# Summing four partial modulation rows with two-column selection matmuls, in place of transposes and a VectorE reduction

## The chip, the cores and the metric

One core of one Trainium2 chip runs the whole program. The time is device microseconds (us) of one execution; beside it stands the profile of one execution, whose span runs from its first to its last instruction. Everything is float32. The weight matrices are split into a high and a low part of a reduced float32 type, so that three fast matmuls stand in for one exact one; the modulation alone uses plain float32 matmuls.

## The reference, cut to what matters

Two layers of a diffusion backbone, 512 latent and 128 context tokens of width 1024. Each layer is modulated by a condition vector: `c` for latent tokens, `c_ctx` for context tokens.

```python
def modulation(cond, w_ada_l, b_ada_l):
    m = jnp.einsum('bd,de->be', jax.nn.silu(cond), w_ada_l) + b_ada_l
    shift, scale, gate = jnp.split(m, 3, axis=-1)
...
    h = x * (1.0 + scale) + shift
    y = mixer(h, ...)               # projections, two attentions, a gated scan, one output projection
    x = layer_norm(DEEPNORM_ALPHA * x + gate * y, ...)
```

`w_ada_l` is 1024 x 3072. What the change touches is how the 3072 values of `m`, for both conditions, come to stand down the 128 partitions, where shift and scale are used.

## The kernel before, in words

The 3072 columns are cut into 12 chunks of 256 for each layer, `j` = 0 to 11 (0 to 3 are shift, 4 to 7 scale, 8 to 11 gate). Chunks 0 to 7 of layer 0 are worked off in pairs at the start (`mod_start`, L1314); the other 16 chunks (4 of layer 0, 12 of layer 1) run later, one at a time, between the projection chunks of the two layers.

For one of these 16, `mod_next` (L297) multiplies the condition (two columns, padded to 32) with the 256 weight columns. The 1024 rows are eight blocks of 128; block `k` goes to the partition group `k % 4` of 32 partitions, and only two blocks are summed in each group. So PSUM holds four partial sums, in the partitions 32q and 32q+1, of two rows of 256 each. ScalarE copies them to `ms` (L305). A later step, `mod_end` (L325), calls `mod_out` (L309): it has to add the four partial sums and turn the row of 256 into two columns of 128 partitions. `mod_out` is called with one chunk at a time, so `n` is 2 in each call.

`mod_start` does the same for its chunks with `sel_c`, a constant of 128 x 2 that is 1 in column c for each partition p with p % 32 == c:

```python
        for i in range(4):
            mm(out=pm[:, 256 + 2 * i:258 + 2 * i], lhsT=ms[:, i // 2, 128 * (i % 2):128 * (i % 2) + 128], rhs=sel_c,
               start=True, stop=True)
```

What it writes is read from PSUM by the `stt` (scalar_tensor_tensor on VectorE, L1323) that adds the bias and stores shift or scale.

The order of the work: generators yield at steps that are priced by hand (`COST`), `drive` picks the next one, and the weight chunks with the modulation chunks between them are the background stream (`bg_stream`, L725, with `MODS` and `ORDER`). `mod_end` of a chunk is called from `flush`, at the end of the next projection chunk or ahead of the next modulation chunk. The framework then writes out a queue for each engine, in which instructions of neighbouring steps may change places; each engine works off its queue in that order. PSUM tiles named `pB` share three banks.

Of the kernel before, what the change touches and what calls it, by code (L numbers as in the profile page):

```python
# [8 lines left out]
F32 = mybir.dt.float32  # L9
# [3 lines left out]
ALU = mybir.AluOpType  # L13
AX = mybir.AxisListType
# [59 lines left out]
def hybrid_kernel(ctx: ExitStack, tc: tile.TileContext, A, cst, outs):  # L74
    nc = tc.nc
# [3 lines left out]
    small = ctx.enter_context(tc.tile_pool(name="small", bufs=2))  # L79
# [5 lines left out]
    def gran(shape=(128, T), dt=F32, name="g"):  # L85
        t = gp.tile(list(shape), dt, tag="g", name=name)
        return t
# [23 lines left out]
    def bankB():  # L111
        return bank("B")
# [10 lines left out]
    mm = nc.tensor.matmul  # L123
    act = nc.scalar.activation
    dve = nc.vector
    tt = nc.vector.tensor_tensor
    stt = nc.vector.scalar_tensor_tensor
# [28 lines left out]
    ident = cs[:, C_ID:C_ID + 128]  # L156
# [3 lines left out]
    sel_c = cs[:, C_SC:C_SC + 2]  # L160
# [126 lines left out]
    modt = [[const.tile([128, KB, 2], F32, name=f"mod{l}{i}") for i in range(3)] for l in range(L)]  # L287
# [21 lines left out]
    def mod_out(l, parts):  # L309
        pm = bankB()  # L310
        n = 2 * len(parts)
        for i in range(n):
            ms = parts[i // 2][1][:, 128 * (i % 2):128 * (i % 2) + 128]
            nc.tensor.transpose(pm[:, 128 * i:128 * i + 128], ms, ident)
        sm = small.tile([128, 4, 2], F32, tag="sm", name="sm")
        v = pm.rearrange("p (i q c) -> p i c q", i=4, q=4)[:, 0:n, 0:2, :]
        dve.tensor_reduce(out=sm[:, 0:n], in_=v, axis=AX.X, op=ALU.add)
        for i, (j, _) in enumerate(parts):
            k0 = 2 * (j % 4)
            b0 = V_BA + 24 * l + 2 * j  # L320
            stt(out=modt[l][j // 4][:, k0:k0 + 2, :], in0=sm[:, 2 * i:2 * i + 2],
                scalar=1.0 if j // 4 == 1 else 0.0, in1=vv[:, b0:b0 + 2].unsqueeze(2).to_broadcast([128, 2, 2]),
                op0=ALU.add, op1=ALU.add)

    def mod_end(l, j, ms):  # L325
        mod_out(l, [(j, ms)])
        if j == 7 and l > 0:
            lg, lb = (vv[:, V_LN + 8 * i:V_LN + 8 * i + 8].unsqueeze(2).to_broadcast([128, KB, 2]) for i in range(2))
            tmp = small.tile([128, KB, 2], F32, tag="lnf", name="lnf", bufs=1)
            tt(out=tmp, in0=scale[l], in1=lb, op=ALU.mult)  # L330
            tt(out=shift[l], in0=shift[l], in1=tmp, op=ALU.add)
            tt(out=scale[l], in0=scale[l], in1=lg, op=ALU.mult)
        if j == 11:
            gt = small.tile([128, 2, KB], F32, tag="gt", name="gt", bufs=1)
            dve.tensor_copy(gt, modt[l][2].rearrange("p k c -> p c k"))
            ps = bankC()
            nc.tensor.transpose(ps[0:16, 0:128], gt.rearrange("p c k -> p (c k)"), ident)
            gr = small.tile([16, 128], F32, tag="gr", name="gr", bufs=1)
            dve.tensor_copy(gr, ps[0:16, 0:128])
            nc.sync.dma_start(out=g_scr[l].rearrange("c (k p) -> (c k) p", p=128), in_=gr)  # L340
# [987 lines left out]
    with in_order(nc.scalar.engine, nc.vector.engine, nc.tensor.engine):  # L1328
        for j in range(4):
# [8 lines left out]
            for k in range(KB):  # L1338
                q = k % 4
                mm(out=ps[32 * q:32 * q + 32], lhsT=sc[:, k, :], rhs=rw[k].rearrange("p s c -> p (s c)"),  # L1340
                   start=(k < 4), stop=(k >= 4))
            ms = gran((128, 2, 256), name="ms0")
# [15 lines left out]
            for i in range(2):  # L1358
                k = 2 * j + i
# [95 lines left out]
```

## Time and profile before

| what | us |
|---|---|
| median of three runs (lowest, highest) | 952.72 (952.40, 954.18) |
| the profiled execution, its own time | 954.79 |
| its span, first to last instruction | 953.0 |
| TensorE busy (PE), and weight loads (PEld) | 901.2, 749.7 |
| VectorE (DVE), ScalarE (ACT), GpSimd (POOL) busy | 596.5, 582.1, 79.3 |

A busy PE is one with a matmul in flight; matmuls overlap, so what a matmul costs is the distance from its start to the start of the next one, not its duration. A plain weight load (LDWEIGHTS) and a matmul (MATMUL) make a pair. The chain that ended last is followed back from the last instruction: its pieces add up to the span, and work outside of it had slack.

### The profile page before, as it was taken

The numbers are of one execution on the slowest core, as the hardware profiler recorded it, in microseconds if no ns is written. First come the engines' busy times: TensorE is split into PE (matmuls) and PEld (weight loads), VectorE is DVE, ScalarE is ACT, GpSimd is POOL, SyncE is SP. The second block draws the span as 40 slices with busy tenths as digits, with TensorE's granted clock in tenths as the row PEclk, the third lists the DMA queues.
The fourth block names the chain that finished last, engine by engine and source line by source line (L and its number), as shares of the span: only waits on it lengthen the run. The fifth ranks groups of instructions, "written<-read, shape, count | busy, mean of one in ns | idle before, by whom it ended". The sixth has DMA issues, their size and how long they took to land.

```text
span 953.0 us, 20559 instructions
## 1 busy us (share of the span) xinstructions
PE 901.2 (95%) x8213; PEld 749.7 (79%) x8213; DVE 596.5 (63%) x1340; ACT 582.1 (61%) x1309; POOL 79.3 (8%) x113
## 2 busy tenths in 40 slices
PE   6999999999999999999999999999989989999995
PEld 3798877887777758678989997878768867777895
DVE  2355557756777865343697466785587795544467
ACT  2335677567776867773265368656877676877311
POOL 0000002000001010200023000020000100210012
PEclk8899999999999999999999999999999999999998
DMA  9946521344431212215614452114124122114222
GB/s 291 315 139 177 150 88 37 104 138 112 128 92 53 91 32 69 70 51 186 208 67 151 114 153 86 29 45 120 51 78 122 47 69 54 51 45 133 77 91 99
DMA packets 103617, 100.37 MB, mean 105 GB/s; under 512 B 9449, under 2 KB 91873, under 8 KB 103521
## 3 DMA queue, kind: packets, MB, share of 16 engines
q1 hardware_dynamic: 103520, 99.05, 35.0%
q8 instruction: 65, 1.06, 0.5%
q14 instruction: 32, 0.25, 0.1%
HBM read 77.25 MB, written 6.31 MB: 88 GB/s over the span
## 4 chain that ended last, share of the span: by engine, by line
PE 70%; DVE 12%; ACT 7%; DMA 7%; issue 2%; SPq 1%; POOL 0%; DVEq 0%; ACTq 0%; POOLq 0%
PE pA L373 8%; PE pA L375 8%; PE pA L374 8%; PE pO L1146 7%; PE pA L394 5%; PE pS L1023 5%; PE pA L395 5%; PE pA L396 5%; DMA wraw<-in_w_in_dram 4%; DMA Q<-Q 2%; PE pS L1027 2%; PE pB L1082 2%; PE pB L1080 2%; PE pB L1079 2%; ACT pS L1031 1%
## 5 line engine op out<-in xcount | busy, mean ns | idle before, releaser
L1030 DVE TENSOR_REDUCE nmx<-pS 128x1 f32<-128x640 f32 x128 | 105.4, 823 | 119.9 <-PE pS L1023 65.3
L373 PE MATMUL pA<-wh,mh 128*128 128x256 f32 x600 | 171.0, 285 | 1.3 <-DVE gate_t L409 1.3
L375 PE MATMUL pA<-wh,ml 128*128 128x256 f32 x600 | 170.3, 284 | 0.0
L374 PE MATMUL pA<-wl,mh 128*128 128x256 f32 x600 | 170.0, 284 | 0.0
L1031 ACT ACTIVATE pS<-pS,nmx 128x640 f32<-128x640 f32 x128 | 98.2, 767 | 50.4 <-DVE nmx L1030 47.5
L260 ACT CAST wh<-wraw 128x512 fp32r<-128x512 f32 x140 | 83.7, 619 | 73.4 <-PE pA L375 31.9
L261 DVE TENSOR_TENSOR wl<-wraw,wh 128x512 fp32r<-128x512 f32 x140 | 92.8, 689 | 39.8 <-ACT wh L260 39.0
L373 PEld LDWEIGHTS pA<-wh,mh 128*128 128x128 f32 x600 | 114.7, 191 | 3.6 <-DVE gate_t L409 2.0
L375 PEld LDWEIGHTS pA<-wh,ml 128*128 128x128 f32 x600 | 114.6, 191 | 1.7 <-issue 1.2
L374 PEld LDWEIGHTS pA<-wl,mh 128*128 128x128 f32 x600 | 114.7, 191 | 1.1 <-issue 0.8
L1088 ACT ACTIVATE PT<-pB 128x512 f32<-128x512 f32 x160 | 89.1, 599 | 27.0 <-PE pB L1080 14.7
L394 PE MATMUL pA<-mh,wh 128*128 128x320 f32 x224 | 71.6, 320 | 0.0
L394 PE MATMUL pA<-hh,wh 128*128 128x320 f32 x224 | 70.6, 315 | 0.7 <-DVE gate_t L409 0.7
L395 PE MATMUL pA<-ml,wh 128*128 128x320 f32 x224 | 70.8, 316 | 0.0
L396 PE MATMUL pA<-mh,wl 128*128 128x320 f32 x224 | 70.6, 315 | 0.0
L396 PE MATMUL pA<-hh,wl 128*128 128x320 f32 x224 | 69.7, 311 | 0.0
L395 PE MATMUL pA<-hl,wh 128*128 128x320 f32 x224 | 69.5, 310 | 0.0
L1146 PE MATMUL pO<-PT,tk 128*64 128x512 f32 x256 | 64.9, 613 | 0.4 <-ACT PT L1088 0.3
L373 PE MATMUL pA<-wh,hh 128*128 128x256 f32 x200 | 57.6, 288 | 0.0
L375 PE MATMUL pA<-wh,hl 128*128 128x256 f32 x200 | 57.0, 285 | 0.0
L374 PE MATMUL pA<-wl,hh 128*128 128x256 f32 x200 | 56.8, 284 | 0.0
L394 PEld LDWEIGHTS pA<-mh,wh 128*128 128x128 f32 x224 | 43.2, 193 | 2.5 <-issue 1.8
(297 smaller groups left out, 1966.3 us busy)
## 6 DMA issues: line engine op xcount, KB each, us to landing
wraw<-in_w_ada_dram SPq DMA_DIRECT2D x32, 512.0 KB, 4.5
wraw<-in_w_in_dram SPq DMA_DIRECT2D x30, 512.0 KB, 4.6
wraw<-in_w_in_dram SPq DMA_DIRECT2D x48, 256.0 KB, 3.4
wa<-in_w_ada_dram SPq DMA_DIRECT2D x32, 256.0 KB, 5.4
wraw<-in_w_out_dram SPq DMA_DIRECT2D x16, 512.0 KB, 3.5
Q<-Q SPq DMA_DIRECT2D x32, 160.0 KB, 2.6
KD<-dkh SPq DMA_DIRECT2D x32, 96.0 KB, 3.2
QD<-dqh SPq DMA_DIRECT2D x32, 80.0 KB, 3.2
```

The source lines that it names most:

```text
L260: nc.scalar.copy(hi[n], src)
L261: tt(out=lo[n], in0=src, in1=hi[n].bitcast(F32), op=ALU.subtract)
L373: mm(out=ps[:, o:o + 256], lhsT=hi[k][:, sl], rhs=a, start=(n == 0), stop=False)
L374: mm(out=ps[:, o:o + 256], lhsT=hi[k][:, sl], rhs=b, start=False, stop=False)
L375: mm(out=ps[:, o:o + 256], lhsT=lo[k][:, sl], rhs=a, start=False, stop=(n == last))
L394: mm(out=ps, lhsT=wa, rhs=hi[k][:, sl], start=(k == 0), stop=False)
L395: mm(out=ps, lhsT=wa, rhs=lo[k][:, sl], start=False, stop=False)
L396: mm(out=ps, lhsT=wb, rhs=hi[k][:, sl], start=False, stop=(k == KB - 1))
L1030: dve.tensor_reduce(out=nmx[:, t, i:i + 1], in_=sv, axis=AX.XY, op=ALU.max, negate=True)
L1031: act(sv, sv, AF.Exp, bias=nmx[:, t, i:i + 1], accum_out=den[:, t, i:i + 1])
L1088: return pt, act(pt, ps, AF.Exp).ins
L1146: x = mm(out=o[64 * (i % 2):64 * (i % 2) + 64], lhsT=value(k, i % 2), rhs=pt, start=k == 0, stop=k == 4)
```

## The change

`mod_out` no longer transposes the two blocks of 128 columns of `ms` into 128 columns of PSUM each and sums four of them on VectorE. It multiplies each block with `sel_c`, so that TensorE makes the sum of the four groups, two columns for each block, and the `stt` reads these columns from PSUM. `sm` and the reduction are gone.

```diff
         pm = bankB()
         n = 2 * len(parts)
         for i in range(n):
-            ms = parts[i // 2][1][:, 128 * (i % 2):128 * (i % 2) + 128]
-            nc.tensor.transpose(pm[:, 128 * i:128 * i + 128], ms, ident)
-        sm = small.tile([128, 4, 2], F32, tag="sm", name="sm")
-        v = pm.rearrange("p (i q c) -> p i c q", i=4, q=4)[:, 0:n, 0:2, :]
-        dve.tensor_reduce(out=sm[:, 0:n], in_=v, axis=AX.X, op=ALU.add)
+            mm(out=pm[:, 2 * i:2 * i + 2], lhsT=parts[i // 2][1][:, 128 * (i % 2):128 * (i % 2) + 128], rhs=sel_c,
+               start=True, stop=True)
         for i, (j, _) in enumerate(parts):
             k0 = 2 * (j % 4)
             b0 = V_BA + 24 * l + 2 * j
-            stt(out=modt[l][j // 4][:, k0:k0 + 2, :], in0=sm[:, 2 * i:2 * i + 2],
+            stt(out=modt[l][j // 4][:, k0:k0 + 2, :], in0=pm[:, 4 * i:4 * i + 4].rearrange("p (k c) -> p k c", c=2),
                 scalar=1.0 if j // 4 == 1 else 0.0, in1=vv[:, b0:b0 + 2].unsqueeze(2).to_broadcast([128, 2, 2]),
                 op0=ALU.add, op1=ALU.add)
```

## Rows read from the trace of the kernel before

**Rows 1.** The page: busy us by engine, granted clock, chain that ended last.
```profile
PE 901.2 (95%) x8213; PEld 749.7 (79%) x8213; DVE 596.5 (63%) x1340; ACT 582.1 (61%) x1309; POOL 79.3 (8%) x113
...
PEclk8899999999999999999999999999999999999998
...
PE 70%; DVE 12%; ACT 7%; DMA 7%; issue 2%; SPq 1%; POOL 0%; DVEq 0%; ACTq 0%; POOLq 0%
```
**Rows 2.** Instructions of L314, L317, L321: ns minimum/median/maximum, first and last start.
```profile
L314 PE MATMUL pB<-cs,ms x32: 270/272/330, 84.0 to 818.5; 128*128 128x128 f32 x32
...
L317 DVE TENSOR_REDUCE sm<-pB x16: 150/166/175, 86.8 to 818.8; 128x4 f32<-128x16 f32 x16
...
L321 DVE SCALAR_TENSOR_TENSOR mod<-sm,vv x16: 150/160/165, 87.0 to 819.0; 128x4 f32<-128x4 f32 x16
```
**Rows 3.** The same view of the start's selection matmuls, L1319 and L1323.
```profile
L1319 PE MATMUL pB<-cs,ms x32: 169/251/251, 15.5 to 54.0; 128*128 128x2 f32 x32
...
L1323 DVE SCALAR_TENSOR_TENSOR mod<-pB,vv x8: 151/156/163, 16.5 to 54.4; 128x4 f32<-128x4 f32 x8
```
**Rows 4.** Chain that ended last, pieces at four calls: start us, us, what.
```profile
132.27 0.22 PE pB L314 x2
...
244.06 0.11 PE pB L314
244.17 0.51 PE pS L1023 x2
244.68 0.11 PE pB L314
...
275.74 0.37 PE pB L314 x2
...
818.54 0.22 PE pB L314 x2
```
**Rows 5.** Timeline of TensorE around one call: start us, us, instruction.
```profile
366.41 0.31 PE L395 MATMUL pA<-hl,wh 128*128 128x320 f32 x1
366.56 0.31 PE L396 MATMUL pA<-hh,wl 128*128 128x320 f32 x1
366.71 0.38 PE L314 MATMUL pB<-cs,ms 128*128 128x128 f32 x2
...
367.07 0.30 PE L395 MATMUL pA<-hl,wh 128*128 128x320 f32 x1
```
**Rows 6.** Timeline of weight loads and matmuls at the start's selection matmuls.
```profile
41.88 0.97 PEld L1319 LDWEIGHTS pB<-cs,ms 128*128 128x128 f32 x8
...
41.99 0.95 PE L1319 MATMUL pB<-cs,ms 128*128 128x2 f32 x8
42.80 0.49 PE L1297 MATMUL pO<-wh,hh 128*128 128x256 f32 x2
```
**Rows 7.** Timeline of TensorE where modulation matmuls follow a call.
```profile
132.11 0.38 PE L314 MATMUL pB<-cs,ms 128*128 128x128 f32 x2
...
132.42 0.85 PE L302 MATMUL pB<-wraw,sc 128*32 128x256 f32 x12
```
**Rows 8.** Timeline of all engines at the second call.
```profile
86.64 0.44 PE L314 MATMUL pB<-cs,ms 128*128 128x128 f32 x2 [1.30 <-ACT ms L305]
...
87.11 0.17 DVE L317 TENSOR_REDUCE sm<-pB 128x4 f32<-128x16 f32 x1
87.20 0.48 DVE L409 TENSOR_TENSOR gate_t<-pA,sge 128x320 f32<-128x320 f32 x1
...
87.74 0.42 PE L394 MATMUL pA<-hh,wh 128*128 128x320 f32 x1 [0.66 <-DVE gate_t L409]
```
**Rows 9.** Chain that ended last: a late call, and a run of small matmuls.
```profile
770.70 0.09 DVE sm L317
...
144.53 0.87 PE pB L870 x61
```
**Rows 10.** Waits of TensorE: total us, times, longest us.
```profile
PE pB L961 <- DVE kst L954: 2.4, 1, 2.4
```

## Prediction

> **What bounds the kernel now.** I read the page first. TensorE has a matmul in flight for 901.2 of 953.0 us, VectorE works for 596.5 and ScalarE for 582.1, and the granted clock stands at its upper level (2.4 GHz) in all but a few slices [rows 1]. Busy time alone doesn't say what sets the end, so the next line is the chain that ended last: 70% of it is TensorE, 12% VectorE, 7% ScalarE, 7% DMA [rows 1]. A microsecond added to TensorE is therefore likely to be paid, and one taken from VectorE likely not to be. Third, the instructions of the touched lines, to know their number and size [rows 2, 3]. Fourth, the chain once more, at each of the 16 calls of `mod_out`, which says where this change can be felt at all [rows 4, 9]. Last, timelines around single calls, which give the cost of a pair as a distance between starts [rows 5 to 8].
>
> At the calls the chain shows this. In 12 of the 16 it runs through the transposes themselves: the first is at 132.27 us, the last at 818.54, and ten have 0.22 us each, as these two have [rows 4]. The call at 275.74 holds 0.37, and one near 430 us holds 0.26. The call at 244 us is split: one transpose, two score matmuls of L1023, then the other transpose, 0.11 us each [rows 4]. The four calls off the TensorE chain are the first two (84.0 and 86.6 us, where VectorE sets the pace), one at 167 us (ScalarE does) and the one at 769.7 us, where a reduction stands in it for 0.09 us [rows 9].
>
> **Removed: the transposes.** A transpose of a block is one pair, since 32 matmuls stand for 16 calls of two [rows 2]. Their price comes from the call at 366.71. Matmuls of L395 and L396 follow each other there at 0.15 us (366.41, 366.56). From the L396 ahead of the transposes to the L395 behind them it is 0.51 us (366.56 to 367.07), and one L394 also lies in between; without the transposes that distance would be two steps of about 0.147, or 0.29. So two transposes cost 0.22 us [rows 5], which is what the chain says as well [rows 4].
>
> **Added: the selection matmuls.** The start of this kernel runs the very same instruction: weights `ms` of 128 x 128, two moving columns, float32. There 16 matmuls in the code are 32 pairs in the trace [rows 3], so a plain float32 matmul is issued as two pairs where a transpose is one. A call will thus issue four pairs in place of two. Eight such pairs have their weight loads in 0.97 us, the last of which takes 0.19, so the loads start (0.97 - 0.19) / 7 = 0.111 us apart [rows 6]. The matmuls say the same: 41.99 to 42.80 us, where the next matmul starts, is 0.81 for eight, with the first two only 0.03 apart. The two columns stream in next to no time; what a pair costs is its load of 128 columns, and only the first load of a call can hide under the matmul ahead of it, as that of the first transpose does now. Four pairs: 4 x 0.111 = 0.445 us. The difference to two transposes is 0.445 - 0.22 = **+0.22 us a call**.
>
> Here the Trainium skill speaks for the change. Its page "TensorE: Matmul & The Clock Gate", section "Back-to-back issue gap", gives matmuls of 1 to 64 columns a floor of about 25 ns and 128 columns 134 cycles (56 ns at 2.4 GHz). As an estimate by that page alone, four pairs cost 0.10 us and two transposes 0.11, and TensorE would lose nothing. The same section warns that its formula leaves weight loads out, and the 0.111 us of this trace, where each matmul brings its own weights, disagrees with 25 ns [rows 6].
>
> **What follows a call.** In 7 calls, 5 of them on the chain, the matmuls of the next modulation chunk (L302) come next, on 32-column weights in another place of the array. They don't start right behind the transposes. The second transpose starts at 132.11 + 0.38 - 0.27 = 132.22, L302 at 132.42: 0.20 us, which holds the streaming of the 128 columns [rows 7]. With two columns the streaming goes: 126 columns at 2.4 GHz are 0.05 us, an estimate. The bounds are nothing and the whole excess over a pair, 0.20 - 0.11 = 0.09. I take 0.05: -0.25 us for five calls (0 to -0.45).
>
> **Removed: the reduction.** 16 reductions of 0.166 us go [rows 2]; where work stands behind one it costs 0.09 us, as from 87.11 to 87.20 [rows 8]. The `stt` stays, and reading PSUM in place of `sm` costs it nothing: 156 ns in the start against 160 [rows 2, 3]. It takes the place of the reduction: the same wait for TensorE, the same release of the `pB` bank. Most reductions stand where VectorE has time to spare. The bounds are 0 and 16 x 0.09 = -1.4 us if every one delayed something on the chain; the chain shows just three pieces of 0.08 to 0.09, and two of them are at 87 us, next.
>
> **The call at 86.64 us** is one where the longer work of TensorE becomes a wait. TensorE has waited 1.30 us for `ms`; the reduction starts at 87.11 when the transposes have ended, behind it in VectorE's queue is L409 (87.20), and TensorE waits for L409 until 87.74 [rows 8]. With four pairs the `stt` starts some 0.22 us later and so does L409: +0.2 us, and the two saved reductions are lost in that wait. At 769.7 us ScalarE waits for the reduction that frees the bank; the `stt` now frees it, so I count nothing (bound -0.09).
>
> No DMA is issued, moved or passed by this change.
>
> **The sum.** 12 calls x 0.22 = +2.66 us; -0.25 for L302; +0.2 at 86.64; together **+2.6 us**. The profiled execution took 954.79 us, of which 953.0 are its span, so 957.4 by that clock, or 1.0027 times. The median of the runs is 952.72; the same factor gives **955.3 us**. The bounds of these terms alone: 2.66 - 0.45 - 0.09 + 0.2 = +2.3 (954.9), less a further 1.2 if all reductions counted (953.8); and 16 x 0.22 = +3.5 if all calls paid (956.2).
>
> A difference under about 0.2% (1.9 us) can't be told from none here; the three runs differ by 1.8 us themselves.
>
> **Rivals.**
>
> *The pairs are paid only in part.* The chain is one path of one execution, and 30% of it is not TensorE [rows 1]. If beside half of the 12 calls another engine holds nearly as long a path, from which TensorE resumes at an unmoved time, the gain or loss is of the order of 6 x 0.22 = 1.3 us: 953.4 to 954.2. Against it: a piece that is added to the longest path lengthens it, whatever runs beside.
>
> *The added pairs are nearly free, and it gets faster.* If the loads of the selection matmuls run under the streams around them, a pair could cost as little as those of the small matmuls of L870, 0.87 us for 61, or 0.014 each [rows 9]. A call would then cost 4 x 0.014 - 0.22 = -0.16 us, 12 of them -2.0, and with the reductions -2.2: 950.5 us. The sign turns where a pair costs 0.055 us, and 0.2% is won below about 0.02. Against it: L870 has weights of 64 x 32 in separate places of the array, while L1319 is the same instruction as the new one and shows 0.111. By the page's 25 ns a pair, an estimate, the change would be worth about zero.
>
> *The queues are written out anew.* The code issues both transposes of a call together, and the queue has two matmuls of L1023 between them at 244 us [rows 4]; so places in the queues depend on what the framework takes an instruction to cost, and both the kind and the number of instructions change here. A matmul moved ahead of one whose input is late costs TensorE a wait; the nearest row is 2.4 us for a single one, L961 for `kst` [rows 10]. One or two such waits more: 957.5 to 960; one fewer: 953 or below. For it is that this shows in the trace at all; against it that the edit is small and each call stays where it is.
>
> **How the numbers follow.** The pairs are paid: 0.50, of it 0.44 above 954.6 us and 0.06 below. Paid in part: 0.25, of it 0.05 above 954.6 and 0.20 within 0.2%. Nearly free: 0.06, of it 0.04 faster and 0.02 within. New queues: 0.19, of it 0.10 slower, 0.04 within, 0.05 faster. Together slower 0.59, within 0.2% 0.32, faster 0.09. The likeliest case has 953.8 to 956.8 as its own range. For 8 in 10 I leave out the two far ends, the nearly free pairs and the worst new waits: 951.8 to 958.0.
>
> **What would show it.** 64 matmuls of 128x2 in the place of 32 of 128x128, 8245 pairs in all, starting 0.11 us apart; chain pieces of some 0.44 us (less where L302 follows) in about 12 calls; no L317; an `stt` of 0.16 us reading `pB`, with VectorE some 1.5 to 2.7 us less busy; L409 later against L305 at the second call. I am wrong if the pairs stand closer than 0.06 us, if the chain leaves TensorE at these calls, or if other instructions than these have changed places and their waits account for the difference.

## Result: 0.6% slower, about 6 us, where 2.6 were forecast

The changed kernel takes 959.72 us (median of 10 runs, 954.53 to 962.34), the kernel before, run beside it, 953.56 (10 runs, 952.35 to 955.02). The ratio is 1.0056, with a 95% interval of 1.0041 to 1.0071. In a second set of 12 runs (new_again, below) it was 1.0047 [1.0031, 1.0063]. The direction was forecast; the time lies 1.7 us above the upper end of the range, that of the second set, 957.72, just inside it. One run of sel_f32r (1070.76 us, clock 0.749) and one of old_4b (1341.45 us, 0.588), both below, stood at a far lower clock than all others and are left out of the ratios.

One caution on the profile after: the profiled execution happens to be the shortest of the ten (954.53 us, span 952.7), so its span can't be set against that of before. The places have to be read one by one.

The page after, as [rows 1]:
```profile
PE 900.4 (95%) x8245; PEld 753.3 (79%) x8245; DVE 593.5 (62%) x1324; ACT 581.0 (61%) x1309; POOL 79.3 (8%) x113
...
PEclk8999999999999999999999999999989999999998
...
q8 instruction: 65, 1.06, 0.5%
...
PE 70%; DVE 12%; ACT 9%; DMA 5%; issue 2%; SPq 1%; POOL 0%; DVEq 0%; ACTq 0%; POOLq 0%
```
The instructions of the changed lines (ns minimum/median/maximum, first and last start), as [rows 2]:
```profile
L313 PE MATMUL pB<-cs,ms x64: 165/251/272, 83.9 to 818.4; 128*128 128x2 f32 x64
...
L318 DVE SCALAR_TENSOR_TENSOR mod<-pB,vv x16: 136/152/163, 86.7 to 818.7; 128x4 f32<-128x4 f32 x16
```
32 more pairs, 16 fewer reductions: the instructions are those forecast. So is their price. TensorE around the call of [rows 5], now 1.8 us earlier:
```profile
364.78 0.31 PE L393 MATMUL pA<-hh,wl 128*128 128x320 f32 x1
364.92 0.50 PE L313 MATMUL pB<-cs,ms 128*128 128x2 f32 x4
365.28 0.39 PE L391 MATMUL pA<-hh,wh 128*128 128x320 f32 x1
365.51 0.31 PE L392 MATMUL pA<-hl,wh 128*128 128x320 f32 x1
```
From the matmul ahead of the call to the second behind it: 365.51 - 364.78 = 0.73 us, against 0.51 with transposes, +0.22 as worked out. The second call, as [rows 8]:
```profile
86.52 0.61 PE L313 MATMUL pB<-cs,ms 128*128 128x2 f32 x4 [1.08 <-ACT ms L305]
...
87.16 0.16 DVE L318 SCALAR_TENSOR_TENSOR mod<-pB,vv 128x4 f32<-128x4 f32 x1 [0.29 <-PE pB L313]
87.24 0.48 DVE L406 TENSOR_TENSOR gate_t<-pA,sge 128x320 f32<-128x320 f32 x1
87.78 0.42 PE L391 MATMUL pA<-hh,wh 128*128 128x320 f32 x1 [0.65 <-DVE gate_t L406]
```
The `stt` does hold up L406: from the start of the call to L391 it is 87.78 - 86.52 = 1.26 us, against 87.74 - 86.64 = 1.10 before [rows 8].

What the forecast didn't have can be seen where the chain that ended last no longer runs through TensorE (start us, us, what). Before, from 131.88 to 139.4 us, it consists of matmuls, and the transposes at 132.27 are among them [rows 4]. After:
```profile
131.86 1.04 PE pB L302 x16
132.91 0.02 issue
132.93 5.61 DMA wraw<-in_w_in_dram
```
A weight load has become the bound there. It is issued when L302 has given its buffer free and takes 5.61 us; the same load took 4.59 in the trace of before. This place alone isn't the loss, though: in old_work_new_order (below), which has the transposes and takes 952.66 us, the chain runs through the same load, 5.88 us from 133.53 us.

### The profile page after: what moved, and what is told of

It reads as the page before. It is cut to its first block, busy times and chain, and to the rows that moved or that the text cites. A ratio compares the mean times of both kernels' runs of the same rounds, so it can differ in the third digit from the quotient of the medians.

```text
span 952.7 us, 20608 instructions
## 1 busy us (share of the span) xinstructions
PE 900.4 (95%) x8245; PEld 753.3 (79%) x8245; DVE 593.5 (62%) x1324; ACT 581.0 (61%) x1309; POOL 79.3 (8%) x113
## 4 chain that ended last, share of the span: by engine, by line
PE 70%; DVE 12%; ACT 9%; DMA 5%; issue 2%; SPq 1%; POOL 0%; DVEq 0%; ACTq 0%; POOLq 0%
PE pA L370 9%; PE pA L372 8%; PE pA L371 8%; PE pO L1143 7%; PE pA L391 5%; PE pA L392 5%; PE pA L393 5%; PE pS L1020 4%; DMA wraw<-in_w_in_dram 3%; PE pB L1079 2%; ACT pS L1028 2%; PE pB L1076 2%; PE pS L1024 2%; PE pB L1077 2%; DVE wl L261 1%
## 5 line engine op out<-in xcount | busy, mean ns | idle before, releaser
L391 PE MATMUL pA<-mh,wh 128*128 128x320 f32 x224 | 71.5, 319 | 0.0
L391 PE MATMUL pA<-hh,wh 128*128 128x320 f32 x224 | 70.5, 315 | 0.7 <-DVE gate_t L406 0.7
L391 PEld LDWEIGHTS pA<-mh,wh 128*128 128x128 f32 x224 | 43.2, 193 | 3.1 <-issue 2.4
```

What stands on the lines that cost most here:

```text
L391: mm(out=ps, lhsT=wa, rhs=hi[k][:, sl], start=(k == 0), stop=False)
```

## Experiments

All but two kernels were written so that the queues of TensorE, VectorE, ScalarE and SyncE keep a recorded order: each instruction gets a dependency on the one that the record has ahead of it, which orders the queue and adds no semaphore.
```
 for i, j in zip(seq, seq[1:]):
     tc.add_manual_dep(j, i.name, mybir.DependencyInfo(NoSync, DATA), reason="pin")
```
"Old order" is that of the kernel before, "new order" that of the changed one. They differ: of 6621 TensorE instructions at most 6297 keep their order among each other. Times are medians, and each ratio is to the kernel before, run beside it in the same set (its medians there are 952.7 to 953.8 us). Code is cut to the lines that change.

**1. Work and order apart.** The four combinations of old and new work with old and new order.

> The changed kernel, with the queues of TensorE, VectorE, ScalarE and SyncE held in the order that they had before the change (the new instructions stand where the old ones stood). Theory P (the pairs are paid, 12 calls x 0.22 less 0.02 at each L302): about +2.5 us on 953.6, so 956.0, ratio 1.0025, and the runs within 3 us of each other as before the change. Theory Q (the new order of the queues brings the stretches at half clock): the same +2.5 us at most, mean granted clock 0.983 to 0.985 in all runs, spread under 3 us. Theory C (the two-column matmuls themselves bring the clock down, in whatever order): like the changed kernel, 957 to 961 us, spread 6 us or more, granted clock between 0.974 and 0.982.

> The kernel before the change, transposes and reductions, with its four queues held in the order of the changed kernel (each reduction just ahead of its scalar_tensor_tensor). Theory P: as before the change, 953 to 954 us. Theory Q: median 955 to 958 us, that is the changed kernel less some 2.5 us of pairs, runs spread over 6 us or more, granted clock from 0.974 to 0.982. Theory C: 953 to 954 us or less, spread under 3 us, clock 0.983 to 0.985.

> The kernel before the change with its four queues held in their own order, as a control of the holding itself: it adds no wait, so all theories expect the time before, 953.6 us within 1 us, spread under 3 us, granted clock 0.983 to 0.985.

> The changed kernel once more, for more executions and another profile. All theories expect 954.5 to 962.5 us, median near 959. Theories Q and C expect time and granted clock to go together, about 1 us for each 0.001 of clock; theory P has no reason for that. If the profile falls on a long execution, the stretches at half clock that it has over the short one show where the time goes.

| | old order | new order |
|---|---|---|
| transposes and reduction | old_pinned 952.93 | old_work_new_order 952.66, ratio 0.9982 [0.9967, 0.9996] |
| selection matmuls | sel_old_order 960.26, ratio 1.0073 [1.0048, 1.0097] | new_again 957.72, ratio 1.0047 [1.0031, 1.0063] |

old_pinned has 0.9997 [0.9982, 1.0012], so the record itself costs nothing. The new order is no loss; its gain, 0.3 us with the old work and 0.5 to 2.5 with the new (959.72 and 957.72 against 960.26), is at the edge of the noise. The new instructions cost 5 to 7 us in either order. So the queues were written out anew, but that is not what cost time.

**2. What of the new work costs it.** All in the old order: `stt` in the place of the reduction; selection with a VectorE copy in that place; transposes written as plain float32 matmuls of 128 columns, so four pairs a call, and the reduction kept; and the selection in reduced float32, which is two pairs a call (`ms_block` stands for a block of 128 columns of `ms`).
```
 sel_copy:    +dve.tensor_copy(sm[:, 0:n], pm[:, 0:2 * n].rearrange("p (i c) -> p i c", c=2))
 plain_ident: -nc.tensor.transpose(pm[:, 128 * i:128 * i + 128], ms, ident)
              +mm(out=pm[:, 128 * i:128 * i + 128], lhsT=ms, rhs=ident, start=True, stop=True)
 sel_f32r:    +ms = small.tile([128, 256], F32R, tag="ms", name="ms")
              +mm(out=pm[:, 2 * i:2 * i + 2], lhsT=ms_block, rhs=selr, start=True, stop=True)
```


> The changed kernel in the queue order of before the change, but with each scalar_tensor_tensor in the place of the removed reduction, not in its own old place (in the run sel_old_order it stood up to 1 us later there and held its pB bank so long). Theory B (of the 7 us of that run some 2 to 3 come from banks held longer): 957 to 958 us at a clock of 0.981 to 0.983. Theory C (the two-column matmuls bring the granted clock down) without B: 960 to 961 us, clock 0.982 or less. Theory P (pairs alone): 955.5 to 956.

> The queue order of before; the transposes become selection matmuls, and the reduction becomes a VectorE copy of the two-column sums to sm in its place, so VectorE keeps as many instructions and the bank is freed where it was. What is left of the change is TensorE's part. Theory P: 955.5 us (+2.5), granted clock 0.984 to 0.986 as before. Theory C: 957.5 to 959, clock 0.979 to 0.982. Theory B has nothing here beyond P.

> The queue order and the VectorE work of before; only the transposes become plain float32 matmuls with the identity, so that a call has four pairs of 128 moving columns. TensorE's time a call is that of the selection matmuls or a little more (0.45 to 0.5 us). Theory P: 955.5 to 956.5, clock 0.984 to 0.986. Theory C: the same 955.5 to 956.5, since the columns keep the array at work, where sel_copy is 957.5 or more with a lower clock. If a lower clock comes with any four pairs, it is not the columns: then 957.5 to 959 here too.

> As sel_early, with ms and the selection constant in the reduced float32 type, so that a selection matmul is one pair: two pairs of two columns a call (the modulation values lose low bits; one small VectorE copy is added at the start). TensorE's time a call is that of the transposes. Theory P: 952.5 to 953.5, clock 0.984 to 0.986. Theory C: 954.5 to 957, clock 0.979 to 0.983, for two columns of work a pair are less than 128.

sel_early took 960.97 us (1.0083 [1.0056, 1.011]), sel_copy 959.88 (1.0077 [1.0046, 1.0108]), plain_ident 960.18 (1.0071 [1.0049, 1.0094]), sel_f32r 949.33 (0.9950 [0.9933, 0.9968]). Four pairs cost 7 us whether they have 2 columns or 128 and whatever VectorE does; two pairs of 2 columns cost nothing. So it is the number of pairs. Theories of the `stt`'s place, of the bank and of the two-column form fell here.

**3. How many pairs, and where.** Unread pairs are added to the old work in the old order: one (one_more), or four (four_ahead), behind the transposes of each call, or two behind L302, there into `ps` (two_behind); `n` stands for 1, 4 or 2. f32r_copy is sel_f32r with the copy of sel_copy.
```
+for _ in range(n):
+    mm(out=pm[:, 256:258], lhsT=identr, rhs=identr[:, 0:2], start=True, stop=True)
```


> The kernel before in its recorded queue order, with one extra pair of two columns per call behind the two transposes (reduced float32, result unread, 16 pairs in all, own time 16 times 0.11 us = 1.8 us, some 1.4 us of it on the path). Theory 'TensorE time alone': about 954.3 us against 952.9 for the pinned kernel without it. Theory 'each 0.11 us in a call is paid more than twice, in proportion' (four pairs cost 7 us more than two, so one more costs 3.5): about 956.4 us. Theory 'a threshold between three pairs and four' (some load or wait that tips over): at most 954 us.

> The kernel before in its recorded queue order, with two extra pairs of two columns for each modulation chunk, but behind its matmuls L302 instead of ahead of them: the same TensorE time as the four-pair kernels, while L302 itself, and with it the release of its weight buffer to the next load, waits no longer in its own chunk. Theory 'late release of the weight buffer': near 955.5 us (952.9 and the 2.6 us of TensorE time). Rival 'any 0.22 us on TensorE at these places costs the same': 960 us like the four-pair kernels.

> The kernel before in its recorded queue order, with four extra pairs per call behind the two transposes (six pairs of TensorE time per call, own time 16 times 0.44 us = 7.0 us, some 5.3 us on the path). Theory 'in proportion': two extra pairs cost 7 us, four cost 14, about 967 us. Theory 'threshold, then TensorE time alone': 7 us for the step and 2.7 for the further two pairs, about 962.6 us. Theory 'TensorE time alone': about 958.4 us.

> The selection in reduced float32 (two pairs of two columns per call; the modulation loses its low bits) with a VectorE copy of the sums where the reduction stood, so that TensorE and VectorE have the numbers of instructions of before. The kernel without the copy took 949.3 us. Theory 'the 3.5 us under the kernel before come from the reduction that is gone': about 952.9 us. Rival 'they come from TensorE's side (two columns instead of 128)': about 949.5 us.

one_more took 956.18 us (1.0024 [1.0006, 1.0042]), two_behind 960.15 (1.0064 [1.0040, 1.0087]), four_ahead 958.29 (1.0046 [1.0029, 1.0063]), f32r_copy 953.36 (0.9991 [0.9974, 1.0008]). Against the kernel before in the same set (953.78), one costs 2.4 us, two cost 6.4, four cost 4.5. One can't be told from its TensorE time alone, 1.3 us, by these intervals; two are well above theirs, 2.7. Four cost no more than two, so it is neither in proportion nor a threshold, and two behind L302 cost what two ahead of it do (7.2 to 8.3 in the four kernels above with four pairs a call), so the release of the weight buffer isn't it either. Four cost just their TensorE time (16 x 0.44 x 12/16 = 5.3): in the trace of four_ahead TensorE is busy 5.1 us longer than in that of old_pinned (907.1 against 902.0) and idle only 0.4 longer.

**4. Earlier loads, no reduction, the reduced selection in its own order.**
```
 old_4b, sel_4b: -wp.tile([128, 4, 256], F32, tag="raw", name="wraw", bufs=3)
                 +wp.tile([128, 4, 256], F32, tag="raw", name="wraw", bufs=4)
                 -GRAN = 49
                 +GRAN = 48
 no_reduction:   -dve.tensor_reduce(out=sm[:, 0:n], in_=v, axis=AX.X, op=ALU.add)
                 -in0=sm[:, 2 * i:2 * i + 2]
                 +in0=pm[:, 4 * i:4 * i + 4].rearrange("p (k c) -> p k c", c=2)
```


> The kernel before in its recorded queue order with a fourth raw weight buffer (and one granule less, 48 instead of 49, for the room): weight loads are issued one buffer earlier, so that ScalarE's casts wait less for them. It is the control for sel_4b. If waits for loads lie on the path in the kernel before, it is faster than the 952.9 us of the three-buffer control by up to the 10 us or so that the casts wait for loads in it, more likely 1 to 3 us; if they don't, 952.9 us.

> The selection kernel in the old queue order (961.0 us with three raw buffers) with the fourth raw buffer and 48 granules. Theory 'the part beyond TensorE's own 2.6 us comes from late weight loads': its distance to old_4b shrinks from 8 us to about 2.6 to 3.5 us. Rival 'it comes from other waits and the clock': the distance stays at 6 to 8 us.

> The kernel before in its recorded queue order, transposes kept, VectorE's reduction left out: the scalar_tensor_tensor reads four columns of the transposed block, so the sums over the four groups are left out of the modulation. Theory 'the reduction costs the old order 3.5 us': about 949.4 us. Rival 'it costs only its place in the queue': about 952.5 us.

> The changed kernel with the selection in reduced float32 (two pairs per call; the modulation loses its low bits), in the queue order written out for it. If the gain in the old order (3.5 us) and the gain of the new order (0.3 to 0.7 us) add, about 948.8 us; if the gain in the old order was an accident of that order, 952 us.

old_4b took 952.14 us (0.9983 [0.9970, 0.9995]), sel_4b 959.48 (1.0064 [1.0045, 1.0084]): the distance of 7.3 us stays though ScalarE's casts wait much less for loads. Late weight loads alone are not it. no_reduction took 951.88 (0.9993 [0.9982, 1.0005]): the reductions are worth some 1 us at most in the old order, not clear of nothing, and within the bound of 1.4. f32r_free took 948.35 (0.9959 [0.9943, 0.9976]).

**5. Waits filled.** Unread matmuls of the identity ahead of long waits of TensorE.
```
+for _ in range(fills[kind].pop(0)):
+    mm(out=ps[:, 0:128], lhsT=identr, rhs=identr, start=True, stop=True)
```


> The kernel before in its recorded queue order, with unread 128-column matmuls of the identity put directly ahead of four waits of TensorE: 10 ahead of the wait of 1.37 us at 256.5 us, 12 ahead of 1.60 us at 422.2, 6 ahead of 0.83 us at 706.6 and 18 ahead of 2.40 us at 781.9. They fit into the waits, so the work on the path stays. Theory 'stretches at the lower clock level follow waits of TensorE': the stretches behind 422, 706 and 782 us go, the time lost to the clock falls from 14 us by 3 to 5, and the kernel takes about 948 to 950 us. Rival 'the lower level comes whatever TensorE did': clock and time stay at 0.985 and 952.9 us, or some tenths more.

> The selection kernel in reduced float32 in its own queue order, recorded (948.4 us unfilled; the modulation loses its low bits), with unread matmuls of the identity ahead of five waits: 6 ahead of 0.85 us at 326.8 us, 5 ahead of 0.70 at 330.3, 12 ahead of 1.60 at 419.4, 6 ahead of 0.84 at 704.3, 28 ahead of 3.91 at 780.0. Theory 'stretches at the lower level follow waits': 3 to 5 us less, about 944 to 945 us, with a clock near 0.988. Rival: 948.4 us and 0.983 as before.

fill_old took 954.39 us (1.0008 [0.9990, 1.0025]), fill_f32r 949.58 (0.9966 [0.9948, 0.9983]). In fill_old the mean granted clock rose from 0.985 to 0.987 and the stretches at the lower level behind 422 and 782 us are gone (that behind 706 stayed, and one at 743 is new), as the theory of the waits has it; the time didn't fall, against it. The trace says why, at a place where nothing was filled (TensorE, old_pinned has no wait here):
```profile
370.33 0.31 PE L402 MATMUL pA<-hh,wl 128*128 128x320 f32 x1
371.84 0.56 PE L1030 MATMUL pS<-k,Q 128*128 128x320 f32 x2 [1.20 <-ACT pS L1038]
```
The same wait stands in sel_old_order, with four pairs and no fillers:
```profile
371.52 1.14 ACT L260 CAST wh<-wraw 128x512 fp32r<-128x512 f32 x2 [1.59 <-DMA wraw<-in_w_in_dram]
...
373.50 0.56 PE L1020 MATMUL pS<-k,Q 128*128 128x320 f32 x2 [1.20 <-ACT pS L1028]
```
Two kernels whose one common change is that TensorE has more instructions meet the same wait of 1.20 us for the same weight load. That led to the cause.

## Where the rest of the time goes: code loading

TensorE's own instructions come by DMA: 65 packets of 16 KB on the queue that the page calls `q8 instruction`. In the trace of after the median number of TensorE's instructions (matmuls, weight loads, and the semaphore instructions between them) from one packet to the next is 256.5. Before and after have the same 65 packets, but not at the same work: each pair is two instructions, so by 716 us the changed kernel has issued 28 pairs, or 56 instructions, more. The packet that before fell at 722.63 us, at instruction 12,716, comes at 716.30, at instruction 12,722.

There it meets a small copy of `Q` that GpSimd and then TensorE wait for. The queues while that copy runs (packets, MB, share), first before, 717.37 to 719.86 us:
```profile
q1 hardware_dynamic: 85, 0.16, 29.4%
```
and after, 715.22 to 718.86 us:
```profile
q1 hardware_dynamic: 83, 0.16, 21.5%
q8 instruction: 1, 0.02, 2.2%
```
The rest of the timeline there, before:
```profile
717.37 0.46 SPq L94 DMA_DIRECT2D Q<-Q  x1
719.86 1.20 POOL L1238 MEMSET Q<- 8x640 f32 x2 [23.57 <-DMA Q<-Q]
```
and after:
```profile
715.22 0.46 SPq L94 DMA_DIRECT2D Q<-Q  x1
718.86 1.20 POOL L1235 MEMSET Q<- 8x640 f32 x2 [25.87 <-DMA Q<-Q]
...
719.54 0.56 PE L1024 MATMUL pS<-k,Q 72*128 72x320 f32 x2 [0.59 <-POOL Q L1235]
```
From issue to memset it was 2.49 us alone and is 3.64 with the code packet between, and TensorE, which didn't wait, now waits 0.59.

The load of the wait at 371 us, in old_pinned (365.28 to 368.70 us) and in sel_old_order (366.57 to 371.52), is the same story:
```profile
q1 hardware_dynamic: 528, 0.52, 45.5%
```
```profile
q1 hardware_dynamic: 528, 0.52, 33.5%
q8 instruction: 1, 0.02, 1.3%
```
The same 528 packets of weights take 3.4 us without and 4.95 us with one packet of code among them.

The third form needs no other DMA. At 743 us TensorE goes through 80 small matmuls, 0.011 us each, so that it uses up instructions many times faster than in its other work. Before, they run in one piece, 0.89 us; after:
```profile
741.20 0.81 PE L867 MATMUL pB<-E,Ei 64*32 64x32 f32 x71
743.13 0.27 PE L867 MATMUL pB<-E,Ei 64*32 64x32 f32 x9 [1.12 <-issue]
```
A wait that no semaphore explains, 1.12 us, with a code packet from 740.70 on. It was read as TensorE short of instructions. The other traces bear that out: in all ten that have this wait it stands behind 13,505 or 13,506 of TensorE's instructions, and it ends 2.25 to 2.43 us after the start of a code packet. In the kernels with the old number of pairs the 80 matmuls are over by instruction 13,466; in four_ahead instruction 13,506 is among them too, but its packet began 2.55 us ahead of the first of them.

All traces, one execution each. "Load" is the weight load of 133 us from issue to landing, in brackets the start of the code packet after its issue; the last columns are TensorE's waits at the three places (us):

| kernel | extra TensorE pairs | load at 133 | 371 | 719 | 743 | time, median |
|---|---|---|---|---|---|---|
| before | 0 | 4.59 (3.96) | 0 | 0 | 0 | 953.56 |
| old_pinned | 0 | 4.62 (3.82) | 0 | 0 | 0 | 952.93 |
| old_work_new_order | 0 | 5.88 (0.28) | 0 | 0 | 0 | 952.66 |
| f32r_copy | 0 | 4.62 (3.89) | 0 | 0 | 0 | 953.36 |
| no_reduction | 0 | 4.57 (3.89) | 0 | 0 | 0 | 951.88 |
| sel_f32r | 0 | 4.38 (3.81) | 0 | 0 | 0 | 949.33 |
| f32r_free | 0 | 4.65 (0.19) | 0 | 0 | 0 | 948.35 |
| old_4b | 0 | 3.41 (none) | 0 | 0 | 0 | 952.14 |
| one_more | 16 | 4.77 (3.85) | 0.81 | 0.95 | 0 | 956.18 |
| two_behind | 32 | 5.40 (0.25) | 0.78 | 1.05 | 0.96 | 960.15 |
| plain_ident | 32 | 6.05 (0.06) | 0 | 0.35 | 0.85 | 960.18 |
| sel_copy | 32 | 5.39 (0.60) | 1.33 | 0.79 | 0.96 | 959.88 |
| sel_old_order | 32 | 5.99 (0.03) | 1.20 | 0.27 | 0.77 | 960.26 |
| sel_early | 32 | 5.69 (0.04) | 1.20 | 0.41 | 0.82 | 960.97 |
| sel_4b | 32 | 4.23 (0.48) | 0 | 0.57 | 1.13 | 959.48 |
| after | 32 | 5.61 (-0.06) | 0 | 0.59 | 1.12 | 959.72 |
| new_again | 32 | 5.50 (-0.14) | 0 | 0.25 | 0.70 | 957.72 |
| four_ahead | 64 | 5.46 (0.66) | 0 | 0.14 | 0 | 958.29 |
| fill_old | 46 | 4.86 (4.23) | 1.20 | 1.02 | 0.82 | 954.39 |
| fill_f32r | 57 | 4.60 (0.09) | 0 | 0.95 | 0.89 | 949.58 |

Eight kernels with the old number of pairs show none of the three waits; every kernel with another number shows some. fill_old has 28 extra pairs behind it by 719 us, just as many as the kernels with 32, and it meets the same waits there and at 743. At 371 us the link is complete: in the six kernels that wait there the packet begins 0.75 to 1.93 us after the load is issued; in the other fourteen it begins ahead of the load or 3.3 us or more behind its issue. At 719 it is as close: in the eleven kernels in which the packet begins 0.95 to 1.87 us after the copy of `Q` is issued, the memset starts 3.35 to 4.23 us after that issue and TensorE waits 0.25 to 1.05; in the other nine it starts after 2.41 to 2.50 us, and only four_ahead has a wait, 0.14. At 133 us a packet at the load's start goes with 5.39 to 6.05 us in nine kernels of three buffers, but with 4.60 and 4.65 in two, so the start alone doesn't decide, and old_work_new_order shows that 5.88 us there need not lengthen the whole. four_ahead fits: with 64 more pairs the packets miss the places at 371, 719 and 743, and what is left is its TensorE time.

## Why the prediction was off, point by point

**Right.** The pair at 0.111 us and +0.22 us a call (0.73 against 0.51). Two pairs for a plain float32 matmul (64 for 32). The chain through TensorE at the calls. "Nearly free" fell: a pair with its own 128 columns of weights costs 0.11 whether 2 or 128 columns stream; the Trainium skill's floor of 25 ns ("TensorE: Matmul & The Clock Gate", section "Back-to-back issue gap"), whose formula leaves weight loads out, is not what such a pair costs here. "Paid in part" fell too: with the pairs, TensorE is busy 2.8 us longer in the old order (below). The +0.2 at 86.64 us came to 1.26 - 1.10 = 0.16.

**Small misses.** L302 starts 0.18 us after the last pair where 0.15 was assumed (0.20 less 0.05), so that term is -0.1, not -0.25. VectorE is 3.0 us less busy where 1.5 to 2.7 were forecast. The chain's pieces at a call are mostly 0.34 us, not 0.44. And the range's +2.3 us is 955.0, not 954.9.

**The step that failed** is the sentence "No DMA is issued, moved or passed by this change", which put the DMA side at nothing. 32 pairs are 64 instructions, and they move the points at which TensorE's code is loaded against the work. The old order shows it best, since the two profiled executions there have the same mean clock and nearly their kernels' median times (952.83 and 959.60 us). First old_pinned, then sel_old_order:
```profile
core 0: 951.0 us, clock 0.983
PE 902.0 (95%) x8213; PEld 750.4 (79%) x8213; DVE 596.6 (63%) x1340; ACT 581.6 (61%) x1309; POOL 78.9 (8%) x113
```
```profile
core 0: 957.8 us, clock 0.983
PE 904.8 (94%) x8245; PEld 753.4 (79%) x8245; DVE 594.9 (62%) x1324; ACT 581.7 (61%) x1309; POOL 79.2 (8%) x113
```
Of the 6.8 us between them TensorE is busy for 2.8, as forecast for the pairs (2.66), and idle for 4.0 (53.0 against 49.0). The new waits make up 3.6 of these: 1.20 + 0.27 + 0.77 = 2.2 us at the three places, and 1.34 us at 140 us behind the load of 133 us.

In the new order the account isn't closed. The trace of after has 0.59 + 1.12 = 1.7 us of such waits beside its 2.66, but its span of 952.7 us, at clock 0.982, is that of old_work_new_order's trace, 952.6 at 0.982: this execution made up for them elsewhere. The median of the changed kernel is 5.1 to 7.1 us above the old work in the same order (957.72 and 959.72 less 952.66), and no trace shows one of its longer executions.

For code loading the Trainium skill has a rule: "Runtime: NRT & Kernel Launch", section "Instruction fetch mechanics", says that code comes in blocks of 16 KiB, 256 instructions, and that crossing a block is mostly hidden. The sizes agree with this trace. That it is hidden holds for most of the 65 packets, not for those that meet a load on which TensorE waits: the copy at 719 is 1.15 us longer, the load at 371 about 1.5.

**What stays open.** The time also goes with the mean granted clock of a run: time times (1 minus clock) is 14.9 us for before (mean of its 129 runs beside the experiments 953.3 us, clock 0.9844) and 20.1 for the changed kernel (mean of 10 runs 958.9 us, 0.9790). By this measure alone, which is the most that the lower level can have cost, 5.3 us lie there, so it overlaps with the pairs and the waits. Such a stretch, as this one after, stands at 0.50, the lower of the two levels, 1.2 GHz (TensorE busy, then other engines, clock, DMA share, GB/s):
```profile
166.00:168.30 2.30, 1.74 (x15) 1.59 (x14) 1.71 (x5) 2.19 (x8) 0.73 (x1) 1.00 0.03 7
168.40:171.70 3.30, 3.30 (x23) 1.44 (x24) 1.69 (x6) 1.06 (x3) 0.00 (x0) 0.50 0.17 47
```
It begins just behind a wait of 0.56 us of L313, and most of the others in or just behind waits of 0.5 to 2.4 us. New waits would thus bring new stretches, and fill_old's clock fits that. So do the traces in which such a stretch begins just behind one of the waits above: at 142.6 to 145.0 us in sel_old_order, sel_copy, sel_early and plain_ident, behind the wait at 140, and at 743.5 to 751.7 in sel_copy, sel_early, plain_ident and fill_old, behind that at 743; no kernel with the old number of pairs has one at either place. But it is not shown how much of the changed kernel's 5 to 7 us is the waits and how much the clock. Nor has it been tried to pad its code so that its packets fall where they did; fill_old and four_ahead move the packets, but with other work. Why sel_f32r is 3.6 us below old_pinned, where the reductions left out give 1.0 and the reduced pairs with a copy nothing, is open as well.

## What to carry over

Where TensorE is the bound, price an edit by pairs with their own weights, 0.11 us each here, and prefer a form with one pair (a transpose, reduced float32) to plain float32 with two, however few columns stream. Then allow for another 0 to 5 us from an edit that changes the number of instructions, as seen here: it moves all later code loads, and a load or a small copy with no slack that one of them met was 0.9 to 1.8 us longer; look in the trace for the `instruction` packets beside the DMAs that the chain waits for. Where the low bits can be spared, the selection in reduced float32 in its own order is the version that beats both kernels: 948.35 us, 0.9959 [0.9943, 0.9976], though why is open.

## What was not expected of the hardware

One 16 KB packet of code (0.88 to 2.97 us on its DMA engine, over all traces) went with a 512 KB weight load of 4.95 us in place of 3.4, and with a copy of `Q` of 3.64 us in place of 2.49. Twice the extra work didn't cost more: 16, 32 and 64 added pairs cost 2.4, 6.4 and 4.5 us. And filling TensorE's waits raised the granted clock (0.985 to 0.987) without making the kernel faster.
